# Re-ordering the opening of a transformer block by token tile

## The chip, the cores and the metric

The kernel runs on one core of one Trainium2 chip. The metric is device microseconds of one execution, the median of several. Engines are named as in the profile: PE is TensorE's matmul stream (PEld its weight loads), DVE is VectorE, ACT is ScalarE, POOL is GpSimd, and SP is the SyncE queue from which all DMAs of this kernel are issued. Each engine takes its own instructions strictly in the order in which they stand in the program.

## What is computed

One block: a first gated feed-forward network (FFN 1), a mixer (differential attention beside a causal convolution), and a second FFN, each on a normalised input that is shifted and scaled by vectors made from a conditioning vector `c`. The tokens are 256, the model width is 2048, the FFN width 5632. The part that matters here is the start:

```python
c_act = jax.nn.silu(c)                                   # (1, 2048)
ada = jnp.einsum('bd,de->be', c_act, w_ada[l]) + b_ada[l]  # 9 vectors of 2048
sh1, sc1, g1, ... = jnp.split(ada, N_MOD, axis=-1)
h = modulate(rms_norm(x, ffn1_norm[l]), sh1, sc1)        # h * (1 + scale) + shift
x = x + 0.5 * g1[:, None, :] * swiglu(h, ffn1_w_gu[l], ffn1_w_down[l])
...
def swiglu(h, w_gu, w_down):
    g, u = jnp.split(jnp.einsum('bsd,df->bsf', h, w_gu), 2, axis=-1)
    return jnp.einsum('bsf,fd->bsd', jax.nn.silu(g) * u, w_down)
```

All inputs and weights are float32. So nothing of FFN 1 can be multiplied before three things have arrived from memory: `x` (for the norm), two columns of `w_ada` for the input dimensions in question (scale and shift), and weights.

## The kernel before

**Tiles.** The 256 tokens are two token tiles of 128 (t = 0, 1; the change's name counts them 0 and 1 too, so "x of tile 1" is the second half of `x`). The 2048 input dimensions are 16 rows of 128 (k = 0 to 15); four rows are one piece. The gate and up columns of FFN 1 are 22 chunks of 512 columns (c = 0 to 21). One weight row of one chunk is 128x512 floats, 256 KB.

**Three matmuls per product.** For accuracy every float32 operand is split in two: ACT casts it to a reduced format (`whi`, the high part), DVE subtracts that from the original (`wlo`, the low part). A product of one weight row with one token tile (`mm3`) is then three matmuls of 128x512: high by high, high by low weight, low by high weight. A split weight row thus feeds six matmuls, three for each token tile. The split of two weight rows is one ACT cast of 128x1024 and one DVE subtraction of 128x1024.

**The conditioning vectors.** `w_ada` is stored transposed: its block j (128 output columns by 2048, 1 MB) is multiplied by the broadcast `c_bc` and summed along 2048 by one DVE instruction. Blocks 2k and 2k+1 are the scale and the shift of row k. ACT and DVE then make the activations of row k from the transposed, normalised `x` in PSUM (`Norm.tile`: one ACT instruction writes the high part, two DVE instructions the low part). Only after that can PE use row k. The two blocks for one row of activations are as much transfer as eight weight rows.

**The opening.** Since activations come row by row, FFN 1 first multiplies only some rows of the first weight piece of each chunk (`EXT`: one row for chunks 0 to 7, two for 8 to 11, three for 12 to 14, four for the others), puts the partial sum into `parts[c]` by an ACT copy from PSUM, and adds the rest later. `LOADS` says which chunks share a DMA. `AGAIN` lists chunks whose missing rows of the first piece follow in a pass of their own, with a DVE addition to `parts[c]` (`add_part`); `EARLY` lists the groups of chunks that go on with the second piece after that. `FIRST_ADA`, and after it `DUE`, say how many `w_ada` blocks are asked for by the time so many weight rows have been loaded. The pools that limit how far ahead work can run are: 6 PSUM accumulators, 4 `whi` and 4 `wlo` tiles of 128x1024, and 4 `raw` tiles of 1 MB, shared by weights and `w_ada` blocks. Eight DMAs can be outstanding: each issue waits until the eighth before it has landed.

**What sets the order.** A scheduler of the tile framework lays out each engine's instructions from the program's text, with priorities by program order and dependencies; `tc.issue_after(i)` keeps what is inside behind instruction i. In the changed kernel `tc.manual_schedule` keeps the instructions of ACT, DVE and PE in the very order in which they are written.

**The order in DMAs before.** SP issues `small`, both tiles of `x`, three half blocks of `w_ada` for row 0, the first weight row, the fourth half block, one weight row, two weight rows, and then `w_ada` blocks and pairs of weight rows in turn.

## Time and profile before

| | us |
|---|---|
| median of 3 runs (1849.39 to 1851.69) | 1849.96 |
| the profiled execution's own time | 1848.81 |
| its span, first to last instruction | 1847.0 |
| PE busy | 1820.2 (99%) |
| DVE busy | 1442.0 (78%) |
| ACT busy | 911.9 (49%) |
| DMA, HBM read | 492.37 MB, 268 GB/s over the span |

The profile is of one execution. Times in it count from the start of the span. A row of the timeline gives the start, the duration, the engine, the line of the kernel, the operation, what it writes and reads, how many such instructions were merged into the row, and in brackets how long the engine was idle before it and what released it. The view of windows gives, for stretches of time, the busy time of each engine with its instructions in brackets, and then the granted TensorE clock, the busy share of the DMA engines, and GB/s. Matmuls overlap in the pipeline, so a row's duration is longer than the distance to the next one, and it is the distance that counts.

### The profile page before, as it was taken

The page shows a single profiled execution, that of the slowest core. Times are in us where ns is not written, and L with a number is a line of the kernel's source. Part 1 is how long each engine was busy: PE and PEld are TensorE (multiplying, and loading weights), DVE is VectorE, ACT ScalarE, POOL GpSimd, SP SyncE. Part 2 cuts the span into 40 slices and gives each one's busy share as a digit, 9 for nine tenths or more (in the row PEclk, how much of TensorE's full clock was granted, in tenths as well). Part 3 has the DMA queues.
Part 4 walks back from the last instruction along what each step waited for, and adds up shares of the span by engine and source line. Part 5 has one row for each costly group of instructions (what it writes and reads, how often), then busy time and mean ns, then how long its engine had stood idle before and what let it go on. Part 6 is the DMA issues. An engine that isn't in the chain of part 4 may idle for free.

```text
span 1847.0 us, 21889 instructions
## 1 busy us (share of the span) xinstructions
PE 1820.2 (99%) x8247; PEld 1501.6 (81%) x8247; DVE 1442.0 (78%) x1922; ACT 911.9 (49%) x1378; POOL 26.5 (1%) x29
## 2 busy tenths in 40 slices
PE   6999999999999999999999999999999999999999
PEld 5788888888888887878888888888888888888887
DVE  7789969998888777899999668878877765544443
ACT  6553444444444433554777655664444444433332
POOL 0000000000000000000110000000000000000000
PEclk8999999999999999999999999999999999999999
DMA  9888968888899898765544458888777755565552
GB/s 381 348 316 307 342 254 316 333 308 338 323 346 350 335 357 329 284 228 205 182 160 138 172 216 306 333 328 318 280 279 273 276 191 194 183 211 211 200 210 80
DMA packets 72729, 495.91 MB, mean 268 GB/s; under 512 B 8192, under 2 KB 8624, under 8 KB 15152
## 3 DMA queue, kind: packets, MB, share of 16 engines
q1 hardware_dynamic: 72624, 494.53, 72.1%
q8 instruction: 64, 1.05, 0.2%
q14 instruction: 41, 0.34, 0.1%
HBM read 492.37 MB, written 2.12 MB: 268 GB/s over the span
## 4 chain that ended last, share of the span: by engine, by line
PE 93%; DVE 3%; ACT 1%; DMA 1%; issue 1%; POOL 0%; SPq 0%; POOLq 0%; DVEq 0%; ACTq 0%
PE acc L317 30%; PE acc L318 30%; PE acc L316 30%; DVE blk L772 1%; PE tp L589 1%; DVE wlo L297 1%; DMA blk<-in_w_gu_dram 1%; PE acc L864 1%; PE tp L378 1%; DMA blk<-in_w_ada_dram 1%; ACT whi L295 0%; PE acc L903 0%; DVE raw L182 0%; ACT blk L469 0%; PE tp L813 0%
## 5 line engine op out<-in xcount | busy, mean ns | idle before, releaser
L295 ACT CAST whi<-raw 128x1024 fp32r<-128x1024 f32 (+1 forms) x605 | 628.4, 1046 | 737.5 <-PE acc L318 613.6
L297 DVE TENSOR_TENSOR wlo<-raw,whi 128x1024 fp32r<-128x1024 f32 (+1 forms) x605 | 725.7, 1212 | 318.3 <-ACT whi L295 316.9
L316 PE MATMUL acc<-whi,blk 128*128 128x512 f32 x2448 | 957.0, 393 | 5.8 <-ACT blk L387 2.2
L317 PE MATMUL acc<-wlo,blk 128*128 128x512 f32 x2448 | 956.7, 391 | 4.6 <-DVE wlo L297 4.6
L318 PE MATMUL acc<-whi,blk 128*128 128x512 f32 x2448 | 956.1, 391 | 0.1
L316 PEld LDWEIGHTS acc<-whi,blk 128*128 128x128 f32 x2448 | 460.5, 188 | 102.0 <-ACT whi L295 2.8
L317 PEld LDWEIGHTS acc<-wlo,blk 128*128 128x128 f32 x2448 | 460.6, 188 | 101.1 <-DVE wlo L297 8.0
L318 PEld LDWEIGHTS acc<-whi,blk 128*128 128x128 f32 x2448 | 460.2, 188 | 97.1 <-DVE blk L389 0.9
L182 DVE CUSTOM_DVE_ANT_0 raw<-raw,c_bc 128x2048 f32<-128x2048 f32 x142 | 324.4, 2285 | 5.3 <-DMA raw<-in_w_ada_dram 4.8
L772 DVE SCALAR_TENSOR_TENSOR blk<-blk,cst,blk 128x255 f32<-128x255 f32 (+17 forms) x240 | 97.5, 463 | 0.5 <-ACT blk L770 0.5
L469 ACT COPY blk<-acc 128x512 f32<-128x512 f32 x88 | 49.8, 591 | 60.6 <-PE acc L318 58.8
L581 DVE TENSOR_TENSOR blk<-acc,blk 128x512 f32<-128x512 f32 x88 | 56.9, 683 | 0.3
L318 PE MATMUL acc<-blk,blk 128*128 128x512 f32 x112 | 43.7, 392 | 0.0
L316 PE MATMUL acc<-blk,blk 128*128 128x512 f32 x112 | 43.7, 393 | 0.0
L317 PE MATMUL acc<-blk,blk 128*128 128x512 f32 x112 | 43.7, 390 | 0.0
L297 DVE TENSOR_TENSOR blk<-raw,blk 128x1024 fp32r<-128x1024 f32 x28 | 33.7, 1220 | 1.8 <-ACT blk L295 1.8
L583 DVE TENSOR_TENSOR blk<-blk 128x256 f32<-128x256 f32 x88 | 33.4, 418 | 0.7 <-ACT blk L582 0.7
L582 ACT ACTIVATE blk<-blk 128x256 f32<-128x256 f32 x88 | 32.2, 411 | 0.8 <-DVE blk L581 0.8
L295 ACT CAST blk<-raw 128x1024 fp32r<-128x1024 f32 x28 | 28.8, 1049 | 6.6 <-DMA raw<-in_w_dn_dram 5.3
L335 DVE TENSOR_TENSOR blk<-tp,blk 128x512 fp32r<-128x512 f32 x44 | 30.0, 684 | 2.3 <-ACT blk L334 2.3
L344 ACT ACTIVATE tmp<-xall 128x512 f32<-128x512 f32 x22 | 13.8, 631 | 31.2 <-DVE xall L642 17.8
L334 ACT CAST blk<-tp 128x512 fp32r<-128x512 f32 x44 | 25.3, 580 | 2.4 <-PE tp L589 2.4
(149 smaller groups left out, 662.8 us busy)
## 6 DMA issues: line engine op xcount, KB each, us to landing
raw<-in_w_gu_dram SPq DMA_DIRECT2D x161, 1024.0 KB, 5.2
raw<-in_w_ada_dram SPq DMA_DIRECT2D x142, 1024.0 KB, 5.9
raw<-in_w_dn_dram SPq DMA_DIRECT2D x88, 1024.0 KB, 4.8
raw<-in_w_in_dram SPq DMA_DIRECT2D x40, 1024.0 KB, 4.8
raw<-in_w_out_dram SPq DMA_DIRECT2D x16, 1024.0 KB, 4.8
raw<-in_w_gu_dram SPq DMA_DIRECT2D x8, 768.0 KB, 5.2
blk<-in_w_gu_dram SPq DMA_DIRECT2D x10, 512.0 KB, 14.1
blk<-gate_line SPq DMA_DIRECT2D x6, 512.0 KB, 5.6
```

The lines of the kernel that those rows point to most:

```text
L182: nc.vector.tensor_tensor_reduce(out=raw, in0=raw, in1=c_bc, scale=1.0, scalar=0.0, op0=ALU.mult, op1=ALU.add, accum_out=ada_cols[g][:, j ...
L295: nc.scalar.copy(out=hi[:, :m, :], in_=rw)
L297: nc.vector.tensor_sub(out=lo[:, :m, :], in0=rw, in1=hi[:, :m, :].bitcast(F32))
L316: nc.tensor.matmul(acc, ah, wh, start=start, stop=False)
L317: nc.tensor.matmul(acc, ah, wl, start=False, stop=False)
L318: return nc.tensor.matmul(acc, al, wh, start=False, stop=stop)
L335: nc.vector.tensor_sub(out=lo, in0=tp, in1=hi.bitcast(F32))
L469: last_part[0] = nc.scalar.copy(out=parts[c][:, t, :], in_=accs[t])
L581: nc.vector.tensor_add(out=p[:, t, :], in0=accs[t], in1=p[:, t, :])
L582: nc.scalar.activation(out=p[:, t, :256], in_=p[:, t, :256], func=AF.Silu)
L583: nc.vector.tensor_mul(out=p[:, t, 256:], in0=p[:, t, :256], in1=p[:, t, 256:])
L772: nc.vector.scalar_tensor_tensor(out=y[:, d:], in0=u, scalar=w, in1=y[:, d:], op0=ALU.mult, op1=ALU.add)
```

## The change

The change rewrites the opening of FFN 1 up to chunk 9 and lets the scheduler lay out the rest.

- **DMAs.** SP now issues `small`, `x` of tile 0, the four half blocks of `w_ada`, six weight rows (chunks 0, 1, 2 and 3, 4 and 5), `x` of tile 1, weights of chunks 6 and 7, two `w_ada` blocks (row 1), weights of chunks 8 and 9, of chunk 10, and so on.
- **Square sums.** They are made tile by tile (`begin_sums`), each with two on ACT and two on DVE; before, the four of tile 1 were all on ACT.
- **Products by tile.** Chunks 0 to 7 (the first `BY_TILE = 5` loads) multiply row 0 with tile 0 only; chunks 0 to 5 do so ahead of tile 1's transposes. Then all eight chunks follow with tile 1 from the same split weights. In all of tile 0 but the first chunk the low activation comes ahead of the low weight (`lo_last`).
- **Partial rows.** `EXT` is one row for chunks 0 to 9, two for chunks 10 to 14, four for the others. `AGAIN` has chunks 4 to 7 instead of 4 to 6, and `DUE` is stretched to match.

```diff
-EXT = (1,) * 8 + (2,) * 4 + (3,) * 3
-LOADS = [(0,), (1,), (2, 3), (4, 5), (6, 7)] + [(c,) for c in range(8, NCH)]
-FIRST_ADA = (0, 0, 1, 1, 1, 1, 1, 0, 1, 1, 1, 1)
-AGAIN = [4, 5, 6]
+EXT = (1,) * 10 + (2,) * 5
+LOADS = [(0,), (1,), (2, 3), (4, 5), (6, 7), (8, 9)] + [(c,) for c in range(10, NCH)]
+BY_TILE = 5
+X_BEHIND = 3
+AGAIN = [4, 5, 6, 7]
-DUE = ((19, 8), (55, 16), (107, 24), (150, 32))
+DUE = ((8, 4), (15, 6), (22, 8), (60, 16), (109, 24), (153, 32))
...
-    for t in range(NT):
-        nc.sync.dma_start(out=xall[:, t, :], in_=x_in[t * P:(t + 1) * P, :])
+    def load_x(t):
+        return nc.sync.dma_start(out=xall[:, t, :], in_=x_in[t * P:(t + 1) * P, :])
+
+    load_x(0)
...
+        def begin_sums(self, t):
+            self.done.add((0, t))
+            for n in range(4):
+                square_sum(n, t, self.ss, n % 2 == 1)
+            self.rstd(t)
+
+        def begin_norm(self, t):
+            self.xn = tmp([P, 512])
+            nc.scalar.activation(out=self.xn, in_=x[0][:, t, :], func=AF.Identity, scale=self.r[t])
+
+        def begin_transposes(self, t):
+            for j in range(4):
+                nc.tensor.transpose(self.raws[j][:, t * P:(t + 1) * P], self.xn[:, j * P:(j + 1) * P], ident)
...
+            st.begin_first()
+            st.begin_sums(0)
+            st.begin_norm(0)
+            st.begin_transposes(0)
+            first_modulation()
+            begun[0] = 1
+            split = []
+            for i in range(BY_TILE):
+                split.append(load(i))
+                if i == X_BEHIND:
+                    with tc.issue_after(w_dma[0].ins):
+                        w_dma[0] = load_x(1)
+                rows[0] += len(LOADS[i])
+            last_load = w_dma[0]
+
+            def first(t):
+                st.tile(st.raws[0][:, t * P:(t + 1) * P], tmp([P, P]), (0, slice(t * P, (t + 1) * P)))
+
+            def products(i, t):
+                for c in LOADS[i]:
+                    acc = acc_tile()
+                    mm3(acc, act(0, t), ws[c](0), True, True, i > 0 and t == 0)
+                    if parts[c] is None:
+                        parts[c] = blk([P, NT, 512])
+                    last_part[0] = nc.scalar.copy(out=parts[c][:, t, :], in_=acc)
+
+            with tc.manual_schedule(engines={mybir.EngineType.Activation, mybir.EngineType.DVE, mybir.EngineType.PE}):
+                split[0]()
+                first(0)
+                split[1]()
+                split[2]()
+                products(0, 0)
+                products(1, 0)
+                split[3]()
+                products(2, 0)
+                st.begin_sums(1)
+                split[4]()
+                products(3, 0)
+                st.begin_norm(1)
+                st.begin_transposes(1)
+                first(1)
+                with tc.issue_after(last_load.ins):
+                    ada_due(rows[0])
+                products(4, 0)
+                for i in range(BY_TILE):
+                    products(i, 1)
+                    if i == 2:
+                        load(BY_TILE)
+                begin_ready()
+            for i in range(BY_TILE, len(LOADS) + AHEAD):
...
+                    with tc.issue_after(w_dma[0].ins), tc.issue_after(st.last.ins):
+                        ada_a_share(ext[LOADS[i][0]] * len(LOADS[i]))
                         begin_ready()
```

Lines have moved: the conditioning sum of a whole block is L182 before and L186 now, of a half block L240 and L243; the casts of weights L295 and L309 before, L298 and L314 now, the subtractions L297 and L310 before, L300 and L315 now; `Norm.tile` L387 to L389 and L396 to L398; the copy into `parts` L469 before, L544 (opening) and L485 now; `add_part` L538 and L603. A buffer's number in the rows below tells it apart from others and means nothing else.

**First place: DVE up to the first product.** `adah` holds the half sums for row 0, `ada` the finished scale and shift. Before:

```order
L240 ISA blk_178,adah_169<-blk_178,c_bc 128x1024
L240 ISA adah_169 128x1
L310 TENSOR_TENSOR wlo_184<-blk_181,whi_183 128x512
L240 ISA blk_187,adah_169<-blk_187,c_bc 128x1024
L240 ISA adah_169 128x1
L242 SCALAR_TENSOR_TENSOR ada_168<-adah_169,cst 128x1
L388 TENSOR_SCALAR tmp_191<-tp_146,scales,ada_168 128x256
L389 TENSOR_TENSOR blk_145<-tmp_191,blk_144 128x256
```

Now:

```order
L243 ISA blk_159,adah_150<-blk_159,c_bc 128x1024
L243 ISA adah_150 128x1
L243 ISA blk_162,adah_150<-blk_162,c_bc 128x1024
L243 ISA adah_150 128x1
L245 SCALAR_TENSOR_TENSOR ada_149<-adah_150,cst 128x1
L315 TENSOR_TENSOR wlo_169<-blk_166,whi_168 128x512
L397 TENSOR_SCALAR tmp_191<-tp_129,scales,ada_149 128x128
L398 TENSOR_TENSOR blk_128<-tmp_191,blk_127 128x128
```

The subtraction of the first weight row went behind the last half block, and row 0 is made for 128 tokens instead of 256.

**Second place: ACT around tile 1.** `acc_213` to `acc_245` are the sums of chunks 2 to 5 with tile 0, `blk_185` is the high part of the weights of chunks 6 and 7, `tmp_251` the normalised tile 1 that PE transposes. Now:

```order
L314 CAST whi_180<-blk_178 128x1024
L544 COPY blk_217<-acc_213 128x512
L544 COPY blk_223<-acc_219 128x512
L353 ACTIVATE tmp_225,ss_124<-xall 128x512
L353 ACTIVATE tmp_229,ss_124<-xall 128x512
L314 CAST blk_185<-blk_183 128x1024
L544 COPY blk_243<-acc_239 128x512
L544 COPY blk_249<-acc_245 128x512
L414 ACTIVATE tmp_251<-xall,rstd_233 128x512
L396 ACTIVATE blk_127<-tp_129,ada_149,scales 128x128
```

Before, both tiles' sums and norms stood ahead of every copy. Further down on ACT, `acc_452` is chunk 12 with tile 0, and the activation is the one of row 2:

```order
L298 CAST whi_386<-blk_384 128x1024
L485 COPY blk_466<-acc_452 128x512
L396 ACTIVATE blk_127<-tp_130,ada_149,scales 128x256
L298 CAST whi_409<-blk_407 128x1024
L485 COPY blk_466<-acc_453 128x512
```

**Third place: DVE where `AGAIN` ends and `EARLY` begins.** Before, `acc_890` is chunk 5, `acc_950` chunk 6 (the last of `AGAIN`), and `wlo_984` belongs to the missing rows of chunk 3, the first of `EARLY`:

```order
L538 TENSOR_TENSOR blk_321<-acc_890,blk_321 128x512
L538 TENSOR_TENSOR blk_321<-acc_891,blk_321 128x512
L297 TENSOR_TENSOR wlo_984<-raw_980,whi_982 128x1024
L431 TENSOR_TENSOR blk_875<-tmp_915,blk_874 128x4x128
L431 TENSOR_TENSOR blk_875<-tmp_931,blk_874 128x4x128
L538 TENSOR_TENSOR blk_338<-acc_950,blk_338 128x512
L538 TENSOR_TENSOR blk_338<-acc_951,blk_338 128x512
```

Now `acc_862` is chunk 6, `acc_897` chunk 7 (the last of `AGAIN`), and `wlo_937` belongs to chunk 3:

```order
L603 TENSOR_TENSOR blk_272<-acc_863,blk_272 128x512
L300 TENSOR_TENSOR wlo_895<-raw_887,whi_893 128x512
L186 ISA raw_919,ada_479<-raw_919,c_bc 128x2048
L186 ISA ada_479 128x1
L603 TENSOR_TENSOR blk_278<-acc_897,blk_278 128x512
L603 TENSOR_TENSOR blk_278<-acc_898,blk_278 128x512
L190 TENSOR_TENSOR ada_479<-ada_479,cst 128x2
L442 TENSOR_SCALAR tmp_982<-tp_977,scales,ada_479 128x128
L228 SCALAR_TENSOR_TENSOR scales<-ada_479,cst 128x1
L442 TENSOR_SCALAR tmp_982<-tp_977,scales,ada_479 128x128
L300 TENSOR_TENSOR wlo_937<-raw_933,whi_935 128x1024
```

The split of the first weights of `EARLY` stood ahead of the additions of the last chunk of `AGAIN` and now stands behind them. From matmul 1010 of PE on (of 8205 in each kernel) the order on PE is the same in both, up to buffer numbers.

More of the change, by code (lines that the diff above doesn't have):

```diff
@@ L196, in ada_due @@
     def ada_due(rows):
-        r0, j0 = 0, 2
-        for r, j in DUE:
+        r0, j0 = DUE[0]
+        for r, j in DUE[1:]:
             if rows <= r:
@@ L235, in first_modulation @@
             for h in range(2):
-                between(2 * i + h)
                 wa = blk([P, 1024])
@@ L306, in w_first, with split, mm3 @@
         w_dma[0] = nc.sync.dma_start(out=raw[:, :n, :], in_=w_gu1[cs[0]:cs[0] + n, 0].rearrange("c p n -> p c n")[:, :, :512])
-        hi = whp.tile([P, 2, 512], F32R, tag="whi", name=nm("whi"))
-        lo = wlp.tile([P, 2, 512], F32R, tag="wlo", name=nm("wlo"))
-        nc.scalar.copy(out=hi[:, :n, :], in_=raw[:, :n, :])
-        nc.vector.tensor_sub(out=lo[:, :n, :], in0=raw[:, :n, :], in1=hi[:, :n, :].bitcast(F32))
-        return [lambda j, i=i: (hi[:, i, :], lo[:, i, :]) for i in range(n)]
-    def mm3(acc, a, w, start, stop):
+        hi = blk([P, 2, 512], F32R) if held else whp.tile([P, 2, 512], F32R, tag="whi", name=nm("whi"))
+        lo = blk([P, 2, 512], F32R) if held else wlp.tile([P, 2, 512], F32R, tag="wlo", name=nm("wlo"))
+        def split():
+            nc.scalar.copy(out=hi[:, :n, :], in_=raw[:, :n, :])
+            nc.vector.tensor_sub(out=lo[:, :n, :], in0=raw[:, :n, :], in1=hi[:, :n, :].bitcast(F32))
+        return [lambda j, i=i: (hi[:, i, :], lo[:, i, :]) for i in range(n)], split
+    def mm3(acc, a, w, start, stop, lo_last=False):
         ah, al = a
@@ L316, in mm3 @@
         nc.tensor.matmul(acc, ah, wh, start=start, stop=False)
+        if lo_last:
+            nc.tensor.matmul(acc, al, wh, start=False, stop=False)
+            return nc.tensor.matmul(acc, ah, wl, start=False, stop=stop)
         nc.tensor.matmul(acc, ah, wl, start=False, stop=False)
@@ L389, in tile, with begin_first @@
             self.last = nc.vector.tensor_sub(out=self.hl[k // 4][:, k % 4, ts], in0=hf, in1=hi.bitcast(F32))
-        def begin_both(self):
+        def begin_first(self):
             self.hh[0], self.hl[0] = blk([P, 4, S], F32R), blk([P, 4, S], F32R)
             tps = [tp_tile((P, 2, S)) for _ in range(2)]
-            for t in range(NT):
-                self.done.add((0, t))
-                self.rstd(t)
-                xn = tmp([P, 512])
-                nc.scalar.activation(out=xn, in_=x[0][:, t, :], func=AF.Identity, scale=self.r[t])
-                for j in range(4):
-                    nc.tensor.transpose(tps[j // 2][:, j % 2, t * P:(t + 1) * P], xn[:, j * P:(j + 1) * P], ident)
-            return [tps[j // 2][:, j % 2, :] for j in range(4)]
+            self.raws = [tps[j // 2][:, j % 2, :] for j in range(4)]
+        def begin_sums(self, t):
[9 more added lines that the diff above has]
+                nc.tensor.transpose(self.raws[j][:, t * P:(t + 1) * P], self.xn[:, j * P:(j + 1) * P], ident)
         def piece(self, kb, t, fine=False):
@@ L487, in load, with begin_ready @@
                 if ext[cs[0]] == 1:
-                    ws.update(zip(cs, w_first(cs)))
+                    views, split = w_first(cs, X_BEHIND < i < BY_TILE)
+                    ws.update(zip(cs, views))
+                    if i < BY_TILE:
+                        return split
+                    split()
                 else:
                     ws[cs[0]] = w_tile(w_gu[cs[0], 0], False, (0, ext[cs[0]]), ext[cs[0]] < 4)
+            def begin_ready():
+                while begun[0] < 4 and base + 2 * begun[0] + 2 <= ada_next[0]:
+                    st.tile(st.raws[begun[0]], tmp([P, S]), (begun[0], slice(0, S)))
+                    begun[0] += 1
@@ L492, in ffn @@
             for c in range(NCH):
                 ext[c] = EXT[c] if c < len(EXT) else 4
-            def begin_ready():
-                while begun[0] < 4 and base + 2 * begun[0] + 2 <= ada_next[0]:
-                    st.tile(raws[begun[0]], tmp([P, S]), (begun[0], slice(0, S)))
-                    begun[0] += 1
-            first_modulation(lambda n: load(0) if n == 3 else None)
-            begin_ready()
-            for i in range(len(LOADS) + AHEAD):
-                if i < len(LOADS):
-                    if i:
-                        load(i)
-                    with tc.issue_after(w_dma[0].ins):
-                        if i < len(FIRST_ADA):
-                            ada_until(ada_next[0] + FIRST_ADA[i])
-                            rows[0] += ext[LOADS[i][0]] * len(LOADS[i])
-                        else:
-                            ada_a_share(ext[LOADS[i][0]])
+            st.begin_first()
@@ L746, in block_kernel @@
     norm2 = Norm(96, "n2", sm([P, NT, 4], "ss"))
-    for t in range(NT):
-        for n in range(4):
-            square_sum(n, t, norm1.ss, t == 0 and n % 2 == 1)
     ffn(norm1, w_gu1, w_dn1, 32, (0.78, 32), (0.78, 104), norm_m, AGAIN, EARLY, EARLY_3)
```

14 lines of the change are left out of this document (9 added, 5 removed).

## The prediction

> **What bounds the kernel now.** The windows of the opening come first, since the page has PE at 99% and lets only its first slices fall short.
>
> ```profile
> core 0: us, PE busy (x) PEld busy (x) DVE busy (x) ACT busy (x) POOL busy (x), PEclk, DMA share, GB/s
> 0.00:10.00 10.00, 3.48 (x16) 3.24 (x16) 1.85 (x7) 5.97 (x14) 0.85 (x6) 0.99 0.79 283
> 10.00:20.00 10.00, 4.57 (x13) 3.04 (x14) 8.49 (x18) 5.65 (x13) 1.47 (x1) 0.50 1.03 394
> 20.00:30.00 10.00, 9.34 (x33) 7.15 (x33) 9.34 (x12) 6.46 (x12) 0.00 (x0) 0.82 1.03 414
> ...
> 70.00:80.00 10.00, 10.00 (x46) 8.29 (x45) 7.96 (x10) 6.14 (x8) 0.00 (x0) 1.00 0.83 313
> ```
>
> From 70 us PE is full, so a microsecond gained earlier reaches the end unless a later wait takes it. DMA is full from 10 us, but DVE is nearly full too. Next the timeline: what starts PE, and where PE stands once it is dense.
>
> ```profile
> 6.11 0.63 ACT L344 ACTIVATE tmp<-xall 128x512 f32<-128x512 f32 x1 [1.06 <-DMA xall<-in_x_dram]
> ...
> 10.53 1.23 DVE L240 CUSTOM_DVE_ANT_0 blk<-blk,c_bc 128x1024 f32<-128x1024 f32 x1 [2.23 <-DMA blk<-in_w_ada_dram]
> ...
> 15.47 1.22 DVE L240 CUSTOM_DVE_ANT_0 blk<-blk,c_bc 128x1024 f32<-128x1024 f32 x1
> ...
> 17.05 0.56 ACT L387 ACTIVATE blk<-tp,ada,scales 128x256 fp32r<-128x256 f32 x1 [2.22 <-DVE ada L242]
> ...
> 17.66 0.80 PE L316 MATMUL acc<-whi,blk 128*128 128x512 f32 x1 [2.18 <-ACT blk L387]
> ...
> 21.98 1.04 ACT L309 CAST whi<-blk 128x1024 fp32r<-128x1024 f32 x1 [0.58 <-DMA blk<-in_w_gu_dram]
> ...
> 61.82 0.50 PE L317 MATMUL acc<-wlo,blk 128*128 128x512 f32 x1 [0.53 <-DVE wlo L297]
> ...
> 70.11 0.39 PE L318 MATMUL acc<-whi,blk 128*128 128x512 f32 x1
> ...
> 75.55 0.39 PE L318 MATMUL acc<-whi,blk 128*128 128x512 f32 x1
> ```
>
> The first product waits for the conditioning sums on DVE, and these for DMA. The last two rows are 24 matmuls apart: 5.44/24 = 0.227 us each. Ahead of 61.82 stand 8x6 + 4x12 + 3x18 + 2 = 152 matmuls, 34.5 us at that pace. So **the opening before loses 61.8 - 34.5 = 27.3 us**, nearly all of what can be won.
>
> **The change, part by part.** *When weights arrive.* Three of these rows wait for DMA: 1.20 MB (`small`, `x` of tile 0) are there at 6.1 us, 2.78 MB (both tiles, one half block) at 10.5, 6.97 MB at 22.0. Read by bytes in the new order: half blocks at 7.6, 9.1, 10.5 and 11.9; weight rows at 12.7 to 16.2; `x` of tile 1 (5.92 MB) at 19.1; chunks 6 and 7 at 20.6.
>
> *The start.* With the first half block at 7.6 instead of 10.5, DVE runs the halves at 7.6, 9.1, 10.7 and 11.9, each about 1.2 us. From the last half's start to the activation took 17.05 - 15.47 = 1.6 us: ACT at 13.5. The first matmul was 0.6 later, 0.5 for half the tokens: **14.0 instead of 17.66**. The weight's subtraction that moved behind the last half lies beside ACT.
>
> *The slow clock.* The same windows, finer, with the last matmuls before the first pause, and a stall much later.
>
> ```profile
> 4.65 2.15 PE L137 MATMUL acc<-cst,c_col 128*128 128x128 f32 x10
> ...
> 9.00:10.00 1.00, 0.00 (x0) 0.00 (x0) 0.00 (x0) 1.00 (x4) 0.01 (x1) 0.94 0.90 234
> 10.00:11.00 1.00, 0.00 (x0) 0.00 (x0) 0.47 (x1) 1.00 (x5) 0.00 (x0) 0.50 0.98 401
> ...
> 23.00:24.00 1.00, 1.00 (x4) 0.76 (x4) 0.94 (x1) 1.00 (x3) 0.00 (x0) 0.73 1.02 397
> ...
> 820.50 0.50 PE L317 MATMUL acc<-wlo,blk 128*128 128x512 f32 x1 [1.96 <-DVE wlo L297]
> ...
> 820.00:824.00 4.00, 3.06 (x12) 2.18 (x12) 4.00 (x9) 1.21 (x2) 0.00 (x0) 1.00 0.61 197
> ```
>
> PE ended at 6.8, the clock fell at about 9.9, 3.1 us later, and rose at about 23.5, 5.8 us after the first product. A stall of 2.0 left it up. With the same 5.8, half clock lasts from 14.0 to 19.8 and loses 2.9, as before.
>
> *Tile 0, then the hole.* The durations:
>
> ```profile
> L469 ACT COPY blk<-acc 128x512 f32<-128x512 f32 x30 | 15.9, 599 | 4.7 <-PE acc L318 4.5
> L295 ACT CAST whi<-blk 128x1024 fp32r<-128x1024 f32 x7 | 7.3, 1067 | 4.9 <-DMA blk<-in_w_gu_dram 4.8
> L344 ACT ACTIVATE tmp<-xall 128x512 f32<-128x512 f32 x6 | 3.7, 630 | 1.1 <-DMA xall<-in_x_dram 1.1
> L387 ACT ACTIVATE blk<-tp,ada,scales 128x256 fp32r<-128x256 f32 x4 | 2.3, 563 | 2.9 <-DVE ada L242 2.2 <-DVE scales L224 0.6
> L399 ACT ACTIVATE tmp<-xall,rstd 128x512 f32<-128x512 f32 x2 | 1.4, 719 | 1.7 <-POOL rstd L143 1.7
> ...
> L182 DVE CUSTOM_DVE_ANT_0 raw<-raw,c_bc 128x2048 f32<-128x2048 f32 x9 | 20.6, 2286 | 0.2 <-DMA raw<-in_w_ada_dram 0.2
> L297 DVE TENSOR_TENSOR wlo<-blk,whi 128x1024 fp32r<-128x1024 f32 x7 | 8.5, 1222 | 0.2 <-ACT whi L295 0.2
> L388 DVE TENSOR_SCALAR tmp<-tp,scales,ada 128x256 f32<-128x256 f32 x4 | 2.2, 539 | 0.7 <-ACT blk L387 0.7
> L389 DVE TENSOR_TENSOR blk<-tmp,blk 128x256 fp32r<-128x256 f32 x4 | 1.7, 424 | 0.1
> ```
>
> One behind the other such instructions start some 0.07 earlier. Twelve matmuls of 0.43 bring chunk 3 to 19.4; chunks 4 and 5 take 1.6 more, to 21.0. PE's next work is tile 1's transposes, and they wait for ACT's queue: copy of chunk 3 from 19.8 to 20.4, two square sums to 21.6, the cast for chunks 6 and 7 to 22.6, two copies to 23.7, the norm to 24.4. `x` of tile 1 was there at 19.1: ACT is late, not the DMA. **PE stands from 21.0 to 24.4, 3.4 us**, and the transposes cost 0.4 (four; a group of eight takes 0.8 further on, from 107.74 to 108.53 in the rows for `AGAIN` below).
>
> *Tile 1 and rows 1 to 3.* 6 + 24 matmuls run dense to 31.6. Then DVE and ACT set the pace, for DVE has two whole blocks (4.5) before chunk 8's weights. Followed in the new order: chunk 10's subtraction ends 0.7 after PE wants it (row 1's activation stands behind four copies); chunk 11's 0.7 (a whole block ahead of it); chunks 13 and 14 lose 1.9, since row 2's activation stands on ACT behind chunk 12's copy, and DVE's queue behind that; chunk 15 loses 0.2, row 3 0.85, chunk 16 0.25. Sum 4.6. From chunk 16 on, a chunk is 24 matmuls (5.4) against DVE's two subtractions and a block (4.6): dense.
>
> The opening then loses 14.0 + 2.9 + 3.4 + 0.4 + 4.6 = 25.3, **2.0 less than before**. What the trace doesn't show is how these queues interlock: nothing of the 4.6 (if ACT's copies run earlier) to twice it.
>
> *The end of `AGAIN`.* Here PE was dense before, and this is how:
>
> ```profile
> 107.74 1.04 PE L378 MATMUL tp<-cst,tmp 128*128 128x128 f32 x8
> 108.53 0.48 PE L316 MATMUL acc<-whi,blk 128*128 128x512 f32 x1
> ...
> 108.64 1.36 DVE L426 TENSOR_SCALAR tmp<-tp,scales,ada 128x128 f32<-128x128 f32 x4
> ...
> 111.12 1.22 DVE L297 TENSOR_TENSOR wlo<-raw,whi 128x1024 fp32r<-128x1024 f32 x1
> ...
> 113.45 1.28 DVE L538 TENSOR_TENSOR blk<-acc,blk 128x512 f32<-128x512 f32 x2
> ...
> 57.87 0.39 PE L318 MATMUL acc<-whi,blk 128*128 128x512 f32 x1
> ...
> 112.73 0.39 PE L316 MATMUL acc<-whi,blk 128*128 128x512 f32 x1
> ...
> 58.30 1.26 ACT L469 COPY blk<-acc 128x512 f32<-128x512 f32 x2 [3.13 <-PE acc L318]
> ```
>
> Chunk 3's weights were split at 111.12, the additions followed at 113.45, and PE went on at 112.73. Now the split stands behind the additions of chunk 7, and these wait for its last matmul. After that starts: 0.4 until a reader begins (57.87 to 58.30), 0.6 for the second addition, 0.2, 0.3, 0.2 and 0.3 for the row 7 pieces (four L426 took 1.36), 1.2 for the split: 3.2. PE has 0.2 of that matmul and two high products (0.45) to do. **It stands for 2.5 at least.** Moreover, between the splits for chunks 5 and 3 DVE has 15 us of work (three and a half splits, two blocks, three pairs of additions) against 12.3 of PE, which adds 0 to 0.8; I take 2.9. The same, smaller, between chunks 4 and 5: 2.2 against 1.7 for eight transposes and two products, 0.5. In all 3.4. It costs nothing only if PE arrives later than these queues, and then it has lost that time already.
>
> Further on additions also precede splits, but a chunk or half a chunk ahead of their use: nothing.
>
> **Sum:** -2.0 + 3.4 = +1.4 us on the profiled 1848.8. That execution was 1.1 below the median, 1849.96; the change is put on the median: **1851.4**.
>
> **The rivals.** *The clock falls in the hole between the tiles.* It speaks for it that it fell 3.1 us after the last matmul and the hole is 3.4; against it, that a PE still on half clock at chunk 5 closes the hole to 2.4, and that 2.0 was harmless. From 24.4 half clock would last another 5.8 and lose 2.7, which the waits behind it absorb little of, as ACT's copies follow PE. Time 1854.0, slower. [...]
>
> *The opening goes dense after tile 1.* The six waits sum to 4.6 and hang on ACT's queue being as late as worked out; DVE's 9.3 of 10 us in the window from 20 speaks for them. Without four fifths of them: 1847.7.
>
> *The change brings no earlier start.* If the half blocks, first of their tensor, land no earlier than at 9.4 (the window from 9 us has only 234 GB/s), the start is 1.8 later and nearly all of the 2.0 is gone: 1853.2.
>
> *The end of `AGAIN` is hidden*, PE being late there anyway: 1848.3. Little speaks for it, as PE is dense from chunk 16.
>
> **How the numbers follow.** Forecast 0.52 (its own range 1849.5 to 1853.3, from 2 either way on the opening), the clock 0.20, the dense opening 0.13, no earlier start 0.10, hidden end 0.05. A measurement tells about 0.2% (3.7 us) from no change: faster means below 1846.3, slower above 1853.7. Below lies only the far side of the dense opening, with both stalls small: 0.06. Above lie most of the clock's case (0.12), and a third of the late start and the forecast's edge (0.08): 0.20. The range reaches from the dense opening to the clock: 1847.3 to 1854.8.
>
> **What would show it.** First product at 14.0 (13.5 to 15); PE idle about 3.4 ahead of tile 1's transposes, released by ACT's norm; granted clock 1.0 or 0.5 at 25 us; 146 matmuls done at 58.4; PE idle about 2.9 at 110 us, released by the split of chunk 3 with the additions ahead of it on DVE. Wrong it is if PE is dense at 110 us, or if the hole isn't there.

## The result

| | before | changed | |
|---|---|---|---|
| median, us | 1850.89 | 1856.15 | ratio 1.0025, 95% interval 1.0014 to 1.0035 |
| the profiled execution's own time | 1848.81 | 1856.48 | +7.7 |
| first product of FFN 1 | 17.66 | 14.51 | -3.2 |
| a fixed place of the program (the only wait of PE near 700 us) | 700.80 | 707.42 | +6.6 |

The change made the kernel 0.25% slower; 1851.4 had been forecast, and 1847.3 to 1854.8 as the range. Nearly all of the difference arises ahead of the place near 700 us, from which on both kernels are the same instructions. So that row leaves out what differs by chance behind it, and the experiments below are read by it too. It is of one execution, though, and holds chance of its own: five executions that have the changed kernel's order up to 62 us (its own and those of runs 1, 5, 8 and 9) have the matmul that stands at 62.21 below between 61.05 and 62.72. In runs 5 and 8 one execution each was slow (10534.68 and 2624.1 us); without it their medians are 1852.41 and 1853.44. The row:

```profile
700.80 0.50 PE L317 MATMUL acc<-wlo,blk 128*128 128x512 f32 x1 [0.78 <-DVE wlo L297]
```

```profile
707.42 0.50 PE L326 MATMUL acc<-wlo,blk 128*128 128x512 f32 x1 [0.79 <-DVE wlo L300]
```

The first is of the kernel before, the second of the changed one. The windows of the changed kernel show where PE isn't full, and at what clock (the columns are PE, PEld, DVE, ACT and POOL busy, the granted clock, DMA's share, GB/s):

```profile
0.00:10.00 10.00, 3.62 (x16) 3.28 (x16) 3.29 (x10) 4.86 (x10) 0.44 (x6) 1.00 0.81 283
10.00:20.00 10.00, 6.60 (x17) 4.97 (x18) 7.84 (x15) 5.98 (x9) 1.31 (x1) 0.52 1.03 367
20.00:30.00 10.00, 6.44 (x19) 4.91 (x19) 6.58 (x13) 6.09 (x12) 0.55 (x1) 0.67 1.02 400
...
110.00:120.00 10.00, 7.76 (x28) 5.91 (x27) 9.45 (x19) 5.74 (x10) 0.00 (x0) 0.83 0.88 315
```

PE is busier than before from 10 to 20 us (6.60 against 4.57), and has two bad stretches that the kernel before has not: 20 to 30 us (6.44 against 9.34) and 110 to 120 us, where it had been dense. In both the granted clock is low as well. PE's timeline has the details:

```profile
14.51 0.80 PE L322 MATMUL acc<-whi,blk 128*128 128x512 f32 x1 [1.28 <-ACT blk L396]
...
21.37 0.39 PE L325 MATMUL acc<-wlo,blk 128*128 128x512 f32 x1
25.32 1.12 PE L418 MATMUL tp<-cst,tmp 128*128 128x128 f32 x4 [3.56 <-ACT tmp L414]
26.09 0.78 PE L322 MATMUL acc<-blk,blk 128*128 128x512 f32 x1
26.66 0.63 PE L324 MATMUL acc<-blk,blk 128*128 128x512 f32 x1
...
30.93 0.41 PE L327 MATMUL acc<-whi,blk 128*128 128x512 f32 x1
...
62.21 0.49 PE L326 MATMUL acc<-wlo,blk 128*128 128x512 f32 x1
...
100.71 0.50 PE L326 MATMUL acc<-wlo,blk 128*128 128x512 f32 x1 [0.58 <-DVE wlo L300]
...
112.39 0.39 PE L327 MATMUL acc<-whi,blk 128*128 128x512 f32 x1
112.62 0.61 PE L322 MATMUL acc<-whi,blk 128*128 128x512 f32 x2
115.47 0.50 PE L326 MATMUL acc<-wlo,blk 128*128 128x512 f32 x1 [2.24 <-DVE wlo L300]
...
116.28 0.60 PE L327 MATMUL acc<-whi,blk 128*128 128x512 f32 x1
...
119.67 0.42 PE L326 MATMUL acc<-wlo,blk 128*128 128x512 f32 x1
```

What was late for it, on DVE and ACT:

```profile
8.22 1.23 DVE L243 CUSTOM_DVE_ANT_0 blk<-blk,c_bc 128x1024 f32<-128x1024 f32 x1 [0.76 <-DMA blk<-in_w_ada_dram]
...
20.51 0.69 DVE L350 CUSTOM_DVE_ANT_0 tmp<-xall 128x512 f32<-128x512 f32 x1 [0.21 <-DMA xall<-in_x_dram]
...
22.63 1.04 ACT L314 CAST blk<-blk 128x1024 fp32r<-128x1024 f32 x1 [0.77 <-DMA blk<-in_w_gu_dram]
...
24.53 0.73 ACT L414 ACTIVATE tmp<-xall,rstd 128x512 f32<-128x512 f32 x1
...
109.95 2.28 DVE L186 CUSTOM_DVE_ANT_0 raw<-raw,c_bc 128x2048 f32<-128x2048 f32 x1
...
112.16 1.35 DVE L603 TENSOR_TENSOR blk<-acc,blk 128x512 f32<-128x512 f32 x2
...
114.20 1.82 DVE L300 TENSOR_TENSOR wlo<-raw,whi 128x1024 fp32r<-128x1024 f32 x2
```

The first half block was there at 8.2 us, `x` of tile 1 at 20.5, the weights of chunks 6 and 7 at 22.6, and the norm started at 24.5. The last three rows are DVE at the end of `AGAIN`: a conditioning block, the two additions of chunk 7, and, behind pieces of the next norm (113.43 to 114.20), the split of chunk 3. The hole between the tiles is there (3.56 us, released by the norm, L414), and so are the two waits in `AGAIN` (0.58 and 2.24). From 26.66 to 30.93 ten matmuls take 4.27 us, 0.43 each instead of 0.227, and from 116.28 to 119.67 eight take 3.39: half clock. 62.21 is the 147th product matmul; 62.2 less 146 x 0.227 is 29.1 us, so the opening loses 29.1 against 27.3 before: +1.8, where -2.0 was forecast. `AGAIN` adds 3.0 in waits (115.47 instead of 112.62 + 0.45, and 0.6 sooner) and 1.6 in half clock. Together 6.4 of the 6.6.

In this trace the clock changes on a grid: at 10.48, 20.72, 24.14, 30.96, 116.30 and 119.71 us, that is, 3, 1, 2, 25 and 1 steps of 3.41 us apart. Windows cut on that grid, of the changed kernel:

```profile
20.72:24.14 3.42, 1.04 (x5) 0.54 (x3) 1.85 (x7) 2.65 (x7) 0.55 (x1) 1.00 1.01 374
24.14:27.55 3.41, 2.23 (x8) 1.94 (x9) 1.77 (x4) 1.58 (x4) 0.00 (x0) 0.50 1.01 409
27.55:30.96 3.41, 3.41 (x10) 2.64 (x9) 3.41 (x3) 1.76 (x3) 0.00 (x0) 0.50 1.04 420
30.96:34.38 3.42, 3.42 (x17) 2.81 (x15) 0.95 (x4) 2.79 (x5) 0.00 (x0) 1.00 1.02 417
112.88:116.30 3.42, 1.18 (x6) 0.69 (x5) 3.42 (x8) 2.30 (x5) 0.00 (x0) 1.00 0.97 350
116.30:119.71 3.41, 3.41 (x10) 2.64 (x9) 3.15 (x8) 1.58 (x4) 0.00 (x0) 0.50 0.81 274
119.71:123.12 3.41, 3.41 (x17) 2.82 (x16) 2.56 (x3) 2.58 (x4) 0.00 (x0) 1.00 0.92 312
```

The steps with 1.04 and 1.18 us of PE work are followed by one at half clock; those full of work by one at full clock; the one with 2.23 leaves the clock as it is. None of these steps was idle throughout: one a third full was enough for the clock to fall.

### The profile page after: what moved, and what is told of

Read it like the earlier page. It is cut to its first block, busy times and chain, and to the rows that moved or that the text cites. A ratio compares the mean times of both kernels' runs of the same rounds, so it can differ in the third digit from the quotient of the medians.

```text
span 1854.7 us, 21880 instructions
## 1 busy us (share of the span) xinstructions
PE 1824.5 (98%) x8247; PEld 1503.8 (81%) x8247; DVE 1443.7 (78%) x1928; ACT 910.9 (49%) x1373; POOL 26.5 (1%) x29
## 4 chain that ended last, share of the span: by engine, by line
PE 91%; DVE 4%; DMA 2%; ACT 1%; issue 1%; POOL 0%; SPq 0%; POOLq 0%; DVEq 0%; ACTq 0%
PE acc L326 29%; PE acc L327 29%; PE acc L322 29%; DVE wlo L300 1%; PE tp L655 1%; DVE blk L835 1%; DMA blk<-in_w_gu_dram 1%; PE acc L927 1%; DVE raw L186 1%; ACT whi L298 0%; PE tp L387 0%; DMA raw<-in_w_ada_dram 0%; DMA blk<-in_w_ada_dram 0%; DVE blk L603 0%; PE acc L966 0%
## 5 line engine op out<-in xcount | busy, mean ns | idle before, releaser
L298 ACT CAST whi<-raw 128x1024 fp32r<-128x1024 f32 x607 | 629.9, 1047 | 732.5 <-PE acc L327 593.1
L300 DVE TENSOR_TENSOR wlo<-raw,whi 128x1024 fp32r<-128x1024 f32 x607 | 727.7, 1213 | 300.9 <-ACT whi L298 299.4
L186 DVE CUSTOM_DVE_ANT_0 raw<-raw,c_bc 128x2048 f32<-128x2048 f32 x142 | 324.2, 2285 | 16.6 <-DMA raw<-in_w_ada_dram 16.3
L485 ACT COPY blk<-acc 128x512 f32<-128x512 f32 x72 | 41.6, 593 | 60.8 <-PE acc L327 58.4
L647 DVE TENSOR_TENSOR blk<-acc,blk 128x512 f32<-128x512 f32 x88 | 56.7, 683 | 0.2
L300 DVE TENSOR_TENSOR blk<-raw,blk 128x1024 fp32r<-128x1024 f32 x28 | 33.7, 1219 | 1.9 <-ACT blk L298 1.9
L298 ACT CAST blk<-raw 128x1024 fp32r<-128x1024 f32 x28 | 28.8, 1050 | 7.7 <-DMA raw<-in_w_dn_dram 6.5
L603 DVE TENSOR_TENSOR blk<-acc,blk 128x512 f32<-128x512 f32 x38 | 24.9, 685 | 7.4 <-PE acc L327 7.4
L445 ACT ACTIVATE tmp<-tp,ada,scales 128x128 f32<-128x128 f32 x36 | 14.8, 458 | 28.5 <-DVE tmp L442 14.6
```

The costliest lines, as they stand in the source:

```text
L186: nc.vector.tensor_tensor_reduce(out=raw, in0=raw, in1=c_bc, scale=1.0, scalar=0.0, op0=ALU.mult, op1=ALU.add, accum_out=ada_cols[g][:, j ...
L298: nc.scalar.copy(out=hi[:, :m, :], in_=rw)
L300: nc.vector.tensor_sub(out=lo[:, :m, :], in0=rw, in1=hi[:, :m, :].bitcast(F32))
L485: last_part[0] = nc.scalar.copy(out=parts[c][:, t, :], in_=accs[t])
L647: nc.vector.tensor_add(out=p[:, t, :], in0=accs[t], in1=p[:, t, :])
```

## The experiments

Theory after the result: the forecast's waits were right, and what it missed is that both waits pull the clock down, together some 4 us. Rivals: whatever PE wins or loses before 38 us is taken up by its later waits for split weights; and, for the wait at the end of `AGAIN`, not the additions are to blame but the amount of DVE's work there. The table holds what was measured; "row" is the place near 700 us in the profiled execution.

| run | median, us | ratio to before, 95% interval | row, us |
|---|---|---|---|
| changed kernel | 1856.15 | 1.0025, 1.0014 to 1.0035 | 707.42 |
| 1 e1, `AGAIN` split first | 1854.91 | 1.0024, 1.0014 to 1.0034 | 705.44 |
| 2 e2, norm ahead | 1854.52 | 1.0022, 1.0012 to 1.0031 | 706.06 |
| 3 e3, hole filled | 1855.79 | 1.0029, 1.0017 to 1.0041 | 705.78 |
| 4 e4, kernel before, kept warm | 1851.48 | 1.0003, 0.9994 to 1.0012 | 702.54 |
| 5 f1, split ahead of block too | 1852.62 | 1.0009, 1.0000 to 1.0019 | 704.70 |
| 6 f4, hole and `AGAIN` filled | 1852.39 | 1.0008, 0.9998 to 1.0017 | 703.41 |
| 7 k1, `AGAIN` filled by half | 1853.04 | 1.0014, 1.0005 to 1.0023 | 703.41 |
| 8 h1, `AGAIN` of three | 1853.53 | 1.0014, 1.0005 to 1.0023 | 704.90 |
| 9 g1, `DUE` sooner | 1856.26 | 1.0030, 1.0018 to 1.0042 | 707.02 |
| 10 f2, norm, filling, split | 1850.57 | 0.9997, 0.9987 to 1.0007 | 702.14 |
| 11 f3, and row 2 ahead | 1850.95 | 1.0002, 0.9992 to 1.0011 | 702.27 |
| 12 g3, f2 with `DUE` sooner | 1852.43 | 1.0010, 1.0001 to 1.0018 | 704.16 |

**1. The split of the next weights ahead of the additions.**

```diff
             w = w_tile(w_gu[g, 0], False, (ext[g], 4))
+            add_held()        # add_part of the chunk before, behind this split on DVE
...
-            add_part(g, accs)
+            held_adds.append((g, accs))
```

> Edit: the changed kernel, with the additions of each AGAIN chunk put behind the split of the next weights on DVE; nothing else. The theory (PE waits for a split that stands behind additions, and the wait lets the clock fall): PE idle ahead of chunk 3's first low-weight product falls from 2.24 us to 0.5 or less, the one between chunks 4 and 5 from 0.58 to 0.3 or less, the granted clock stays 1.0 from 110 to 125 us, and the median comes 2.5 to 4 us lower, 1852.2 to 1853.7. The rival (chunk 3's weights land too late anyway, their cast began only at 110.1 us): the idle time stays at 1.5 or more and the median within 1 us of the changed kernel's 1856.15.

The 0.58 went. The 2.24 became 2.21, and the clock fell there. But not for the rival's reason: the cast of chunk 3 ended at 108.0, four microseconds ahead of the split; neither range held the median, 1854.91. PE's row, and what DVE did instead:

```profile
113.44 0.50 PE L326 MATMUL acc<-wlo,blk 128*128 128x512 f32 x1 [2.21 <-DVE wlo L300]
```

```profile
108.41 2.28 DVE L186 CUSTOM_DVE_ANT_0 raw<-raw,c_bc 128x2048 f32<-128x2048 f32 x1
...
112.17 1.82 DVE L300 TENSOR_TENSOR wlo<-raw,whi 128x1024 fp32r<-128x1024 f32 x2
```

A whole conditioning block and four norm pieces (110.61 to 112.04) stood ahead of the split, and DVE never waited. Taking the additions away took next to nothing off the wait: the place is short of DVE time, and block and pieces alone make the split as late. Of the 2.0 us by the row, 1.2 are no doing of this edit: the matmul at 62.21 stood at 61.05 already, where the order is the changed kernel's, as half clock lasted one step of the grid behind the hole here and two there.

**2. Tile 1's norm behind its square sums on ACT.**

```diff
                 st.begin_sums(1)
-                split[4]()
+                st.begin_norm(1)
                 products(3, 0)
-                st.begin_norm(1)
                 st.begin_transposes(1)
                 first(1)
+                split[4]()
...
```

> Edit: the changed kernel, with tile 1's norm put on ACT right behind its square sums (ahead of the cast for chunks 6 and 7 and of two copies), and chunks 6 and 7 multiplied last. The theory (ACT's queue, not the DMA, holds tile 1): the norm starts at 22.9 instead of 24.53 us, the hole shrinks from 3.6 to about 2.1 us, tile 1's first product is at 25.0 instead of 26.09, and the clock falls there in fewer executions; median 1.1 to 4 us lower, 1852.2 to 1855.0. The rival (from chunk 10 on PE waits for split weights, so whatever is won before 38 us is lost there): PE's idle time from 38 to 63 us grows by what the hole gives up, and the median stays within 0.7 of 1856.15.

```profile
23.85 0.66 PE L418 MATMUL tp<-cst,tmp 128*128 128x128 f32 x4 [2.17 <-ACT tmp L414]
25.17 0.50 PE L322 MATMUL acc<-whi,blk 128*128 128x512 f32 x1 [0.66 <-ACT blk L396]
```

The hole shrank to 2.17 and the first product of tile 1 came at 25.17 instead of 26.09, as the theory had it. The norm started at 23.07 (22.9 was expected), and it now waited for the square sums of `x`, which had landed at 20.64: what is left of the hole is not ACT's order. The row near 700 came 1.4 us sooner, so the later waits did not take back the 0.9. The rest fits the clock, which fell in the shorter hole as well but stayed down for one step of the grid (26.47 to 29.89), not two.

**3. The hole filled with unread matmuls.**

```diff
                 st.begin_norm(1)
+                warm = acc_tile()
+                for _ in range(14):
+                    nc.tensor.matmul(warm, act(0, 0)[0], ws[5](0)[0], start=True, stop=True)
                 st.begin_transposes(1)
```

> Edit: the changed kernel, with 14 matmuls of chunk 5's operands into an unread PSUM tile between tile 0's last product and tile 1's transposes; they keep PE busy in the hole and move nothing else. The theory (the hole costs twice, once as idle time and once because the clock falls in it): tile 1's first product stays at 26.1 us, but the granted clock is 1.0 from 24 to 31 us in all executions, and the 12 matmuls at half pace give back 2.6 us in the executions that had them; what is left is the fall at 116 us. Median 1.5 to 3 us lower, 1853.1 to 1854.7. The rival (PE runs into the same weights at 38 us whatever the clock): the clock is up, but the waits from 38 to 63 us grow by as much, and the median stays within 0.7 of 1856.15.

The clock stayed up from 21 to 114 us and the row came 1.6 us sooner, though tile 1's transposes were 0.9 later in this execution (26.26). The median hardly moved, 1855.79: the clock fell after the wait in `AGAIN`, and once more near 820 us, where the kernel before has a wait of 1.96 us too and the clock falls in some executions and not in others. The median alone would have called this one for the rival.

**4. The kernel before, kept warm ahead of its first product.** 36 transposes of constants went into PE's three pauses.

```diff
+            ins = warm_up(22, None)     # and 5 and 9 more behind the two groups of transposes
             for t in range(NT):
```

> Edit: the kernel before, with 36 matmuls on constants in PE's pauses from 6.8 to 17.4 us, so that its clock doesn't fall ahead of the first product. If the slow clock at the start is a cost by itself, as the prediction has it (2.9 us in either kernel), the granted clock is 1.0 at the first product (still 17.66 us) and the time is 2 to 2.9 us under the kernel before. The rival (DVE was 9.3 to 9.9 of 10 us busy from 20 to 50 us in the kernel before, so the splits set the pace and PE only waits longer): the clock is 1.0, yet the time is within 1 us of the kernel before.

```profile
17.57 0.50 PE L316 MATMUL acc<-whi,blk 128*128 128x512 f32 x1 [1.65 <-ACT blk L387]
17.90 0.39 PE L317 MATMUL acc<-wlo,blk 128*128 128x512 f32 x1
18.13 0.39 PE L316 MATMUL acc<-whi,blk 128*128 128x512 f32 x1
...
28.02 0.49 PE L316 MATMUL acc<-whi,blk 128*128 128x512 f32 x1 [2.52 <-ACT blk L480]
```

Full clock from the first product, and nothing won: PE stood 2.52 us at 28 us instead, and the clock fell there. From 40 us on PE waits where it waited before and as long, and the row 61.82 of the kernel before stands at 61.95. The 1.7 us by which the row near 700 is later arise behind that, where the clock fell once more (62.88 to 66.29). In the kernel before, DVE and ACT set the pace of the opening, and the slow clock at its start is hidden. The rival was right.

**5. The split ahead of the block and the pieces too.**

```diff
-            ada_a_share(n)
-            pieces(last_part[0])
+            held_n.append(n)            # both behind the next weights' split, with the additions
```

> Edit: as in the run with the splits first, and moreover each AGAIN chunk's conditioning block and its norm pieces are put behind the next weights' split on DVE. There the additions had gone behind the split, but PE still stood 2.21 us, with a whole block and four pieces of norm ahead of the split on DVE. The theory now (what stands ahead of that split is DVE's amount of work, 2.3 us a block, not the additions' wait for PE): PE's idle time ahead of chunk 3's first low product falls under 0.4 us, the clock stays 1.0 from 105 to 125 us, and the median is 3 to 4.5 us under the changed kernel, 1851.6 to 1853.2. The rival (DVE is behind altogether, so the block that was moved makes the next split late): a wait of 1.5 us or more appears between 113 and 140 us instead, the clock falls there, and the median is 1854.3 or more.

```profile
117.88 0.66 PE L387 MATMUL tp<-cst,tmp 128*128 128x128 f32 x4 [0.91 <-ACT tmp L445]
118.82 0.50 PE L326 MATMUL acc<-wlo,blk 128*128 128x512 f32 x1 [0.28 <-DVE wlo L300]
```

No wait at chunk 3 and no fall of the clock; 1852.62, within what was expected. Waits of 0.91 and 0.28 appear one chunk later, where DVE does what was put off: part of the rival, without its size. PE is 2.7 us ahead at 700 (3.2, counted from 62 us).

**6. Both waits filled, none removed.** As in 3, with nine such matmuls ahead of chunk 3's first product.

> Edit: the changed kernel with 14 unread matmuls in the hole between the tiles and 9 more ahead of chunk 3's first product; no wait is removed, PE is only kept busy in both. It prices the clock alone. The theory: the split of chunk 3 still comes at 115 us less what the hole's clock gave back, the granted clock is 1.0 from 22 to 800 us, and the median is 3 to 4 us under the changed kernel, 1852.2 to 1853.2. The rival (the slow clock costs nothing, because PE meets later waits in any case): the clock is 1.0 and the median is 1855.3 to 1856.5.

```profile
110.00:120.00 10.00, 9.80 (x43) 7.80 (x42) 10.00 (x19) 6.70 (x12) 0.00 (x0) 1.00 0.87 312
```

The clock is 1.00, the split of chunk 3 comes where DVE lets it, and the kernel is 3.8 us faster than the changed one by the median and 4.0 by the row. That is the price of the clock alone, out of a loss of 5.3 by the median. (By the row it holds the chance of the opening: this run passes the place of 62.21 at 59.81, the five executions with the clock down in the hole 1.2 to 2.9 later.)

**7. The wait in `AGAIN` filled by half.** Four matmuls instead of nine.

> Edit: as in the run with hole and AGAIN filled, but only 4 unread matmuls (0.9 us) instead of 9 ahead of chunk 3's first product, so that about half of the wait of 2.24 us stays as idle time. In the runs so far the clock changed only on a grid of 3.41 us, and fell at the end of a grid step in which PE was busy for 0.49 or less; 0.52 and more left it up. By that rule an idle time of about 1.3 us can't bring a step under 0.6, whatever its phase: the granted clock stays 1.0 at 113 to 125 us, the row near 700 us stands within 0.4 of 703.4, and the median is within 0.6 of the 1852.4 measured with 9. The rival (a fall needs only a pause of some length, or the 9 matmuls helped by something else than the clock): the clock still falls there, the row stands near 705.5 and the median is 1854.5 or more.

```profile
113.07 0.50 PE L326 MATMUL acc<-wlo,blk 128*128 128x512 f32 x1 [1.33 <-DVE wlo L300]
```

```profile
112.26:115.67 3.41, 2.60 (x11) 2.17 (x12) 3.41 (x8) 2.99 (x7) 0.00 (x0) 1.00 0.83 271
115.67:119.09 3.42, 3.42 (x16) 2.82 (x15) 3.42 (x6) 2.81 (x4) 0.00 (x0) 1.00 0.80 304
```

PE stands 1.33 us, its step of the grid is 2.60 of 3.41 full, and the clock stays. The row near 700 is the same as with nine, 703.41. (The median is 0.65 above that run's, a hair more than the 0.6 that was written.) The pause that left three quarters of its step full (2.60 of 3.41) brought no half clock; the changed kernel's, which left a third (1.18 of 3.42), cost 1.6 us more.

**8. `AGAIN` of three chunks**, `AGAIN = [4, 5, 6]`.

> Edit: the changed kernel with AGAIN of chunks 4 to 6, as before the change. On DVE the additions of chunk 6 stand ahead of chunk 3's split, and no block stands between them. The prediction's step gives a wait of 2.2 to 2.5 us there, one chunk sooner than in the changed kernel, and the clock falls in most executions: median 1855 to 1856.5, no better than the changed kernel. If the fourth chunk and the block that goes with it are the cause, the wait is under 1.0 us and the median 1852 to 1853.5.

```profile
110.30 0.50 PE L326 MATMUL acc<-wlo,blk 128*128 128x512 f32 x1 [1.46 <-DVE wlo L300]
```

```profile
107.74 1.37 DVE L603 TENSOR_TENSOR blk<-acc,blk 128x512 f32<-128x512 f32 x2 [0.39 <-PE acc L327]
```

Here the additions alone stand right ahead of chunk 3's split: 1.46 us, and the clock stayed up. DVE waits 0.39 for PE ahead of them, and from the last matmul of `AGAIN` (107.99) to PE's next low-weight product pass 2.31 us. This is the prediction's step without its pieces: 0.4 + 0.6 + 1.2 there, 2.2 in all, and a wait of 1.55. Neither range of this run held it. With run 1 (block and pieces alone: 2.21), the changed kernel (all: 2.24) and run 5 (none: nothing at that place) the wait has two causes, each enough for most of it, and the block with its pieces is the larger; block and pieces were not tried apart.

**9. `DUE` sooner**, 16 blocks by row 50 instead of 60.

> Edit: the changed kernel with one number undone: DUE asks for 16 blocks by row 50 instead of row 60, so that two more conditioning blocks (2.3 us of DVE each) are summed before AGAIN, where DVE still has pauses, and two fewer inside it; the additions of chunk 7 stay ahead of chunk 3's split. If DVE's amount of work in AGAIN makes the split late, PE's idle time ahead of chunk 3's first low product falls from 2.24 us to under 1.0, the clock stays up there, and the median is 3 to 4 us under the changed kernel: 1852.2 to 1853.2. If the prediction's step is right as it stood (the additions wait for chunk 7's last matmul, then two additions and a split: 0.4 + 1.3 + 1.2 less 0.45), 2.2 to 2.5 us remain, the clock falls there in most executions, and the median is 1854.5 to 1856.

```profile
80.50 0.73 PE L322 MATMUL acc<-whi,blk 128*128 128x512 f32 x2 [1.62 <-ACT whi L298]
```

The wait at chunk 3 is gone and the clock stays up at 115, but this doesn't decide between the two cases. A block still stands ahead of the additions (113.29), and from the last matmul of `AGAIN` (115.74) to PE's next low-weight product (118.04) pass 2.30 us, as in run 8; only PE has eight transposes and two more high products to do meanwhile, which the scheduler put there. Earlier, two blocks now follow each other on DVE (73.11 and 75.32), the next weights are split late, and PE stands at 80 us instead. The time is that of the changed kernel.

**10. Norm ahead, rest of the hole filled, split first**: runs 2, 3 (eight matmuls) and 5 together.

> Edit: three edits together: tile 1's norm ahead on ACT, eight matmuls into an unread PSUM tile in what is left of the hole, and the AGAIN splits ahead of block and additions. If the changed kernel loses by its two places of waiting and by the clock that falls at them, all of this is gone: no granted clock under 1.0 from 25 to 800 us, tile 1's first product at 25.1, and PE about 2.5 us ahead of the changed kernel at 98 us and 6 to 7 ahead after 120; median 1848.6 to 1850.4, level with the kernel before or up to 1.7 under it. If the order by token tile loses by something else, too (waits for split weights from 38 to 63 us that grow), the median stays at 1851.5 or more.

The best of these orders, 5.6 us faster than the changed kernel and no different from the one before. It is 0.2 above the range, and 5.3 us ahead by the row where 6 to 7 were expected. The clock is 1.00 from 25 us on. It passes the place of 62.21 2.1 us sooner, at 60.10 (the wait just before it stands at 57.90 instead of 60.01), which makes the opening's loss 27.0 against 27.3: with both waits mended, the order by token tile is worth 0.3 us in this execution (0.2 and 0.9 in those of runs 11 and 12). What is lost to the kernel before, 1.3 us at 700, is the 0.93 and 0.28 behind `AGAIN`.

**11. Row 2's activation ahead of chunk 12's copy**, in the same kernel.

> Edit: the same three edits, and the copy of chunk 12's first sum put behind row 2's activation on ACT. The forecast charged 1.9 us to this one row: if ACT's order is what delays it, the waits near 47 to 50 us (0.94 and 0.51 in the changed kernel) fall to 0.5 together and the median is 0.5 to 1.2 us under the run without this edit. If the weights of chunks 13 and 14 or DVE's two subtractions set them, the waits stay and the median is within 0.5 of it.

```profile
46.05 0.73 PE L322 MATMUL acc<-whi,blk 128*128 128x512 f32 x2 [0.49 <-ACT whi L298]
...
52.42 0.73 PE L322 MATMUL acc<-whi,blk 128*128 128x512 f32 x2 [0.94 <-ACT whi L298]
```

The median is that of the second case, but the mechanism is that of the first. At chunk 13 the waits fell from 0.94 and 0.51 to 0.49: ACT's order had set them. But the scheduler laid ACT out anew, and the casts for chunk 15 now stand behind the copy of chunk 14's first sum, which waits 1.00 us for PE (at 50.84). So 0.94 and 0.53 open there, at 52 us, and nothing is won.

**12. Run 10 with `DUE` sooner.**

> Edit: tile 1's norm ahead on ACT, eight unread matmuls in what is left of the hole, each AGAIN split ahead of additions, blocks and pieces on DVE, and DUE asking for 16 blocks by row 50. The run with the first three had waits of 0.93 and 0.28 us left behind AGAIN and was level with the kernel before. With the blocks out of AGAIN these should go; PE would be 1.0 to 1.3 us ahead of that run at 700 us, level with the kernel before or 0.3 behind, and the median 1849.0 to 1850.5, within 0.1% of the kernel before. It is a rival's turn if the two blocks that follow each other on DVE near 70 us open a new wait of a microsecond there: then the median is 1850.5 to 1851.5.

The rival, and worse than it was put: the 1.62 us wait of run 9 is there, the clock fell after it (its grid step had 1.43 of 3.41), and run 10 stays the best.

## Why the prediction was wrong

- **The first product earlier: right**, 14.51 for 14.0. The first half block landed at 8.2 instead of 7.6; the rest followed as worked out.
- **The slow clock at the start, 2.9: nearly**, 3.1 here (to 20.8). That it is a cost of the kernel before too was wrong in effect: run 4 took it away and won nothing.
- **The hole: right in size (3.4, measured 3.6), half right in cause.** ACT's queue was late, but so was the DMA: `x` of tile 1 came at 20.5 instead of 19.1 and the weights of chunks 6 and 7 at 22.6 instead of 20.6. Run 2 shows what ACT's order had in it: 0.9 at the first product of tile 1. The rate wasn't at fault: the forecast's rows make 364 GB/s (4.19 MB from 10.5 to 22.0 us), and the window from 10 us had 367. But landing times were read as if transfers came one behind the other. `x` of tile 1, issued at 8.1, should have been there with 5.92 MB; by 20 us the first two windows had moved 6.5 MB, so part of what was issued behind `x` had been moved before it landed.
- **The clock in the hole: the step that failed.** The prediction gave it 0.20, an estimate of its author's, on "3.1 us after the last matmul" and on a stall of 2.0 that "left it up". By the grid, a pause of 3.6 leaves one of the two steps that it touches at least 1.8 us idle, more than half, and the clock fell in all five executions that had this hole as it was (the changed kernel, runs 1, 5, 8 and 9). The 3.1 us were where the grid happened to lie: in this hole the clock fell 2.4 us after the last matmul (21.76 and 24.14). The 2.0 us stall was luck: in six of the runs above the clock fell at that very stall near 820 us (in run 1 its step had 1.47 us of work), in the others not (1.76 in the kernel before). The price given there, 2.7, was near: 2.3 (from 26.09 to 30.93 eleven matmuls take 4.84 us instead of 11 x 0.227).
- **The six waits of rows 1 to 3: right**, 4.6 forecast and 4.7 lost from 38.0 to 62.2 us, where 86 matmuls stand (0.34, 0.34, 0.94, 0.51, 0.17, 0.37 as idle time, the rest in the rows beside the waits, where 38.96 and 39.30, for one, stand 0.34 apart instead of 0.227). For the largest, at chunk 13, run 11 shows the cause that was given, too.
- **The end of `AGAIN`: right in place and nearly in size** (0.5 and 2.9 forecast, 0.6 and 2.4 lost), **and its steps hold:** from chunk 7's last matmul, 112.39, the second addition starts 0.43 later (112.82), the split 1.38 after that and PE 1.27 after the split, 3.08 in all where 3.2 was forecast. What the forecast took for a small addition, DVE's amount of work, is a cause of the same size, though: the block ahead of the additions is done only at 112.2, so that DVE is never idle there, and run 1 shows that without the additions the wait stays. **That the clock falls after it wasn't in the prediction at all**, a term put at nothing without a reason: 1.6 us.
- **The sum.** Forecast +1.4. With the clock held up in both places (run 6) the row stands at +2.6 and the median at 1.0008: the waits were forecast to about a microsecond. In the opening, of the 3.8 us between -2.0 and +1.8, 2.3 are the clock, 0.5 the later start and most of the rest the hole with its transposes. The clock added 4.0 by the row and 3.8 by the median, and carried the time out of the range. (In the rival with the hidden end, 1851.4 less the 3.4 of that wait is 1848.0, not 1848.3.)
- Behind 700 us the profiled execution of the changed kernel loses another 1.0. A pause of 0.63 at 1320 us that the kernel before hasn't takes 0.8 of it; the rest wasn't followed.

## What to carry to other kernels

Price a pause of PE twice: by its length, and by whether it can leave a 3.41 us step of the clock about half empty or more, which cost 1.6 to 2.3 us more here; a few unread matmuls in the pause buy that back without mending the wait. Before a transfer or a sum is moved to a later stage, count the work of the engine that does it in that stage: `AGAIN` had no DVE time left for two more blocks. And an earlier start is worth only what the queues behind it let through: here 3.2 us at the first product were 0.2 to 0.9 at the end of the opening (runs 10 to 12).
